# Output projection and SwiGLU FFN in seven quarter products, three blocks of 704 tokens

## The chip, the cores and the metric

The kernel runs on one core of a Trainium2 chip. The time of a run is the device time in microseconds (us) of one execution; the times of the kernel before were 2599.57, 2597.79 and 2597.86 us, median 2597.86. Engines carry the profile's names: PE is the matrix engine (PEld its weight load), DVE the vector engine, ACT the scalar engine, POOL the GpSimd engine, SP the engine whose queue issues the DMAs.

## What is computed

One inference step of a decoder layer: 2048 new positions and 8 x 8 tokens of running sequences, 2112 tokens in all, width 1024. Two mixers fill the 1024 columns of `y` (S5: 512, HGRN2: 512); the change begins behind them:

```
x  = x + concat([y5, yh]) @ w_out                        # 1024 x 1024
h2 = rmsnorm(x, norm_ffn)
x  = x + (silu(h2 @ w_gate) * (h2 @ w_up)) @ w_down      # 1024 x 2816, twice, and 2816 x 1024
y  = rmsnorm(x, norm_final)                              # x * (mean(x*x) + eps) ** -0.5 * g
```

## The kernel before

All activations are feature-major: features on the 128 partitions, tokens along the free axis. Every product of this part is made in three matmuls: an fp32 operand is split in a high part (`hi`, ACT, L226: a copy to fp32r) and the rest (`lo`, L227: POOL or DVE subtracts), and `mm3` (L256 to L263) adds hi x hi, hi x lo and lo x hi in PSUM. Each matmul takes a 128 x 128 weight tile and streams 256, 320 or 512 tokens.

The first part of the program (u projection, S5, HGRN2, GLU) interleaves generators and writes `y_s` in DRAM; the change leaves it alone. The rest goes by the four token blocks of `GROUPS`: 576 tokens (256 and 320), and three of 512. For each block

- `mix(e, b)` loads x and `y_s`, splits y, loads and splits the eight weight units of `w_out` (`load_unit`), and adds eight products to x (L980);
- `norm2` makes the norm: squares (ACT), their sum (DVE), a one-column matmul per 128 tokens (L999) that leaves one number for each token on the partitions, `inv_rms` (L289, L290), which raises these to the power -0.5 on POOL, and `spread` (L297, L301), which multiplies a diagonal with a matrix of ones to bring the result to all partitions; then x * gain * r, and the split of h;
- `ffn` goes over the 22 column units of the FFN in pairs: gate (L1067), silu (L1070), up, the product s (L1081) and its split (L1083, L1084), and `down` of the pair before, added to x (L1055). A weight is loaded and split anew for each block, as units of 128 x 1024, raw tiles from a pool of four buffers (`raw2`);
- `final` makes the last norm and writes yT.

The mix of the next block runs among the last steps of an FFN, and the final norm of a block among the first steps of the next. The POOL power is written so:

```
nc.vector.tensor_scalar(st[:rows, a:b], ss[:rows, a:b], 1.0 / D, EPS, op0=ALU.mult, op1=ALU.add)
nc.gpsimd.tensor_tensor(r[:rows, a:b], st[:rows, a:b], e.mhalf[:rows, 0:b - a], op=ALU.pow)
```

with at most four columns in one instruction. The program is written in program order; the Tile framework's scheduler then fixes one order for each engine, which the chip keeps.

Of the kernel before, what the change touches and what calls it, by code (L numbers as in the profile page):

```python
# [983 lines left out]
def fm_norm(e, x, n, name):
    nc = e.nc
    acc = raw_tile(e, pool=e.nraws, name=f"sq_{name}")[:, :2 * n]
    acc = acc.rearrange("p (k t) -> p k t", t=n)
    for j in range(0, KD, 2):
        if j == 0:
            nc.scalar.activation(acc, x[:, 0:2], AF.Square)  # L990
            continue
        sq = raw_tile(e, pool=e.nraws, name=f"sq_{name}_{j}")[:, :2 * n].rearrange("p (k t) -> p k t", t=n)
        nc.scalar.activation(sq, x[:, j:j + 2], AF.Square)
        nc.vector.tensor_tensor(acc, acc, sq, op=ALU.add)
    tl = tiles_of(0, n)
    ss = e.ps_x.tile([P, 4], F32, tag="x", name=f"ss_{name}")
    for j, (o, w) in enumerate(tl):
        for a in range(2):
            nc.tensor.matmul(ss[:w, j:j + 1], acc[:, a, o:o + w], e.ones[:, 0:1], start=a == 0, stop=a == 1)  # L999
    return ss  # L1000


def norm2(e, b, x1):
    nc = e.nc
    out = []
    for gi, (t0, n) in enumerate(GROUPS[b]):
        x = cols(x1, b, gi)
        r = e.small.tile([P, 4], F32, tag="r", name=f"r_f{t0}")
        inv_rms(e, fm_norm(e, x, n, f"f{t0}"), tiles_of(0, n), r, f"f{t0}")
        pr = spread(e, r, tiles_of(0, n), f"f{t0}")  # L1010
        pcs = pieces_of(n)
        op = []
        for j, (k, nk) in enumerate(pcs):
            raw = raw_tile(e, pool=e.nraws, name=f"h{t0}_{j}")[:, :nk * n].rearrange("p (k t) -> p k t", t=n)
            for i in range(nk):
                nc.vector.scalar_tensor_tensor(raw[:, i], x[:, k + i], e.gain[:, KD + k + i:KD + k + i + 1], pr[:, :n],
                                               op0=ALU.mult, op1=ALU.mult)
            hi, lo = wtile(e, f"h{t0}_{j}", e.ops)
            flat = raw.rearrange("p k t -> p (k t)")
            split(e, flat, hi[:, :nk * n], lo[:, :nk * n], nc.vector if j % 2 else nc.gpsimd)  # L1020
            op.append((hi, lo))
        out.append((t0, n, op_k(op, pcs, n)))
    return out


def final(e, b, x1, parts=None):
# [1 line left out]
    T0 = GROUPS[b][0][0]
    for t0, n in parts or GROUPS[b]:
        x = x1[:, :, t0 - T0:t0 - T0 + n]  # L1030
        r = e.small.tile([P, 4], F32, tag="r", name=f"r_z{t0}")
        inv_rms(e, fm_norm(e, x, n, f"z{t0}"), tiles_of(0, n), r, f"z{t0}")
        pr = spread(e, r, tiles_of(0, n), f"z{t0}")
        for k in range(0, KD, 2):
            raw = raw_tile(e, pool=e.nraws, name=f"z{t0}_{k}")[:, :2 * n].rearrange("p (k t) -> p k t", t=n)
            for i in range(2):
                nc.vector.scalar_tensor_tensor(raw[:, i], x[:, k + i], e.gain[:, 2 * KD + k + i:2 * KD + k + i + 1], pr[:, :n],
                                               op0=ALU.mult, op1=ALU.mult)
            nc.sync.dma_start(fm(e.o["yT"], k, 2, t0, n), raw)
# [284 lines left out]
```

## Time and profile before

| | |
|---|---|
| profiled execution, own time | 2605.76 us |
| its span, first to last instruction | 2604.0 us |
| median of three runs | 2597.86 us |
| granted PE clock, mean | 0.979 of full |
| PE busy | 2493.2 us, 96% of the span |
| POOL busy | 1284.3 us, 49% |
| DVE busy | 950.5 us, 37% |
| ACT busy | 724.2 us, 28% |
| DMA moved | 325.44 MB, mean 125 GB/s |
| chain that ended last | PE 83%, POOL 7%, DVE 3%, DMA 3% |

A busy share is an average over the span. PE's matmuls are pipelined, and the duration of one in the profile is longer than the step from one to the next: the step is read from start times. The chain that ended last follows the work back from the last instruction, at each step to what released it.

### The profile page before, as it was taken

What the parts mean: (1) busy time and instruction counts of PE and PEld (TensorE: products, weight loads), DVE (VectorE), ACT (ScalarE), POOL (GpSimd) and SP (SyncE); (2) the same over time, 40 slices, a digit from 0 to 9 for tenths busy, and PEclk for the clock granted to TensorE, in tenths of its full rate; (3) what the DMA queues carried; (4) which work ended last, traced back from release to release, by engine and by line L of the source; (5) the groups of instructions that cost most, each with busy time, mean ns of one, the idle gap of its engine ahead of it and who ended that gap; (6) DMA issues with size and microseconds to landing.
All of it is one profiled execution on the core that took longest, in us unless ns stands there. A gap on an engine that the chain in (4) does not pass through costs nothing.

```text
span 2604.0 us, 40679 instructions
## 1 busy us (share of the span) xinstructions
PE 2493.2 (96%) x16597; PEld 2141.9 (82%) x16597; DVE 950.5 (37%) x1896; ACT 724.2 (28%) x1161; POOL 1284.3 (49%) x1220
## 2 busy tenths in 40 slices
...
GB/s 266 183 264 199 176 184 167 140 146 124 161 134 169 67 130 114 87 85 89 82 74 101 187 97 98 85 99 92 185 98 112 90 97 97 130 97 97 97 65 33
DMA packets 185966, 325.44 MB, mean 125 GB/s; under 512 B 73642, under 2 KB 109939, under 8 KB 185779
## 3 DMA queue, kind: packets, MB, share of 16 engines
...
q8 instruction: 130, 2.13, 0.3%
q14 instruction: 58, 0.47, 0.1%
...
## 4 chain that ended last, share of the span: by engine, by line
PE 83%; POOL 7%; DVE 3%; DMA 3%; issue 2%; SPq 1%; ACT 1%; POOLq 0%; DVEq 0%; ACTq 0%
PE pu L263 19%; PE pg L263 19%; PE pd L263 19%; PE po L263 7%; PE ps_v L263 3%; PE ps_u L263 2%; PE pz L263 2%; PE ps_f L263 2%; PE ps_g L263 2%; PE ps_q L263 2%; POOL H L802 1%; POOL t L801 1%; POOL t L800 1%; POOL H L803 1%; POOL H L804 1%
## 5 line engine op out<-in xcount | busy, mean ns | idle before, releaser
L1055 DVE TENSOR_TENSOR x<-x,pd 128x512 f32<-128x512 f32 (+1 forms) x448 | 253.1, 585 | 537.4 <-PE pd L263 536.5
L227 POOL TENSOR_TENSOR l_wd<-r_wd,h_wd 128x1024 fp32r<-128x1024 f32 x88 | 215.5, 2448 | 341.9 <-ACT h_wd L226 328.0
L263 PE MATMUL pg<-h_h,h_wg 128*128 128x512 f32 (+2 forms) x880 | 311.7, 354 | 9.3 <-ACT h_wg L226 9.3
L263 PE MATMUL pg<-h_h,l_wg 128*128 128x512 f32 (+2 forms) x880 | 310.9, 354 | 2.2 <-POOL l_wg L227 2.2
L263 PE MATMUL pd<-hl,h_wd 128*128 128x512 f32 (+2 forms) x896 | 312.1, 349 | 0.6 <-POOL hl L1084 0.6
L263 PE MATMUL pd<-hh,l_wd 128*128 128x512 f32 (+2 forms) x896 | 311.7, 349 | 0.0
L263 PE MATMUL pg<-l_h,h_wg 128*128 128x512 f32 (+2 forms) x880 | 310.9, 353 | 0.0
L263 PE MATMUL pu<-h_h,l_wu 128*128 128x512 f32 (+2 forms) x880 | 309.6, 352 | 1.1 <-POOL l_wu L227 1.1
L263 PE MATMUL pu<-h_h,h_wu 128*128 128x512 f32 (+2 forms) x880 | 309.9, 352 | 0.0
L263 PE MATMUL pu<-l_h,h_wu 128*128 128x512 f32 (+2 forms) x880 | 309.8, 352 | 0.0
L227 POOL TENSOR_TENSOR l_wu<-r_wu,h_wu 128x1024 fp32r<-128x1024 f32 x88 | 213.8, 2429 | 182.5 <-ACT h_wu L226 182.5
L263 PE MATMUL pd<-hh,h_wd 128*128 128x512 f32 (+2 forms) x896 | 296.2, 349 | 0.1
L227 POOL TENSOR_TENSOR l_wg<-r_wg,h_wg 128x1024 fp32r<-128x1024 f32 x88 | 213.0, 2420 | 128.1 <-ACT h_wg L226 125.6
L1081 DVE TENSOR_TENSOR s<-s,pu 128x512 f32<-128x512 f32 (+1 forms) x110 | 65.3, 594 | 460.8 <-PE pu L263 457.9
L226 ACT ACTIVATE h_wd<-r_wd 128x1024 fp32r<-128x1024 f32 x88 | 93.5, 1062 | 434.3 <-PE pd L263 290.8
L263 PEld LDWEIGHTS pg<-h_h,h_wg 128*128 128x128 f32 x880 | 167.3, 190 | 29.9 <-ACT h_wg L226 9.5
L263 PEld LDWEIGHTS pd<-hl,h_wd 128*128 128x128 f32 x896 | 169.0, 189 | 21.5 <-POOL hl L1084 0.8
L263 PEld LDWEIGHTS pg<-h_h,l_wg 128*128 128x128 f32 x880 | 167.0, 190 | 23.2 <-POOL l_wg L227 2.6
L263 PEld LDWEIGHTS pd<-hh,h_wd 128*128 128x128 f32 x896 | 168.3, 189 | 21.0 <-ACT hh L1083 0.3
L263 PEld LDWEIGHTS pd<-hh,l_wd 128*128 128x128 f32 x896 | 168.8, 189 | 19.9
L263 PEld LDWEIGHTS pg<-l_h,h_wg 128*128 128x128 f32 x880 | 167.2, 190 | 20.6
L263 PEld LDWEIGHTS pu<-h_h,l_wu 128*128 128x128 f32 x880 | 165.8, 188 | 21.6 <-POOL l_wu L227 1.4
...
## 6 DMA issues: line engine op xcount, KB each, us to landing
r_wg<-in_w_gate_u SPq DMA_DIRECT2D x88, 512.0 KB, 3.3
r_wu<-in_w_up_u SPq DMA_DIRECT2D x88, 512.0 KB, 3.3
r_wd<-in_w_down SPq DMA_DIRECT2D x88, 512.0 KB, 3.2
r_wo<-in_w_out_u SPq DMA_DIRECT2D x32, 512.0 KB, 3.3
xr_u<-in_xr SPq DMA_DIRECT2D x16, 512.0 KB, 5.3
r_xu<-in_xT SPq DMA_DIRECT2D x14, 512.0 KB, 5.4
r_y<-y_s SPq DMA_DIRECT2D x14, 512.0 KB, 5.5
h_v<-wx_s SPq DMA_DIRECT2D x12, 512.0 KB, 4.3
```

The lines of the kernel that those rows point to most:

```text
L226: e.nc.scalar.activation(hi, raw, AF.Copy)
L227: eng.tensor_tensor(lo, raw, hi.bitcast(F32), op=ALU.subtract)
L263: e.nc.tensor.matmul(out, whl[k][a], xhl[k][b], start=start and i == 0, stop=stop and i == len(seq) - 1)
L800: eng.tensor_tensor(t1, prev, ar.to_broadcast(two), op=ALU.mult)
L801: eng.tensor_tensor(t2, prev, ai.to_broadcast(two), op=ALU.mult)
L802: eng.tensor_tensor(dst, dst, t1, op=ALU.add)
L803: eng.tensor_tensor(dst[:, 0], dst[:, 0], t2[:, 1], op=ALU.subtract)
L804: eng.tensor_tensor(dst[:, 1], dst[:, 1], t2[:, 0], op=ALU.add)
L1055: nc.vector.tensor_tensor(x1[:, d, o], x1[:, d, o], ps[:, :n], op=ALU.add)
L1081: nc.vector.tensor_tensor(s[:, :n], s[:, :n], pu[:, :n], op=ALU.mult)
```

## The change

The tokens go in three blocks of FT = 704, each in two halves of FH = 352. `w_out`, `w_gate`, `w_up` and `w_down` are each taken as 2 x 2 quarters: two row tiles of the output (j and j + 4, or two FFN units) by two halves of the contraction, against the two halves of the contraction by the two token halves. Seven products of quarters (the Winograd form of Strassen's scheme) take the place of eight, each with the three matmuls of hi and lo. What this needs:

- `w_prep` loads a raw weight pair into one of two raw tiles (pool `wr`, two buffers), makes four sums on DVE, and splits seven operands of 128 x 512, hi on ACT and lo on POOL, into a ring of `ws` pairs (7, later 10);
- `combine` makes the four sums of the activations on DVE; y, h and s go with their sums to DRAM as seven slots (`ty_s`, `h_s`, `s_s`), and `x_slots` loads and splits them into a ring of X pairs (7, later 8), lo on DVE;
- `seven` runs the products, two matrices in turn, in three PSUM tiles for each matrix (A, Q, B), of which A and B go on summing after a sink has read them; the sinks add to x, or make silu and the product;
- `norm_r` sums the squares with a full 128 x 128 matmul of ones, so that each partition has the sums of all tokens, and raises [128, 704] to the power -0.5 in one POOL instruction. `inv_rms` and `spread` are no longer used here;
- the order of the program: mix of all three blocks with norm2 of the block before in between, then the FFN of the three blocks, with `final` of the block before after 14 of the FFN's steps (two units of gate and up).

The diff, cut:

```diff
+FT = 704
+FH = FT // 2
+CH = [(0, 4), (8, 4), (16, 3)]
...
+def combine(v, t, b11, b12, b21, b22):
+    v.tensor_tensor(t[0], b12, b11, op=ALU.subtract)
+    v.tensor_tensor(t[1], b22, t[0], op=ALU.subtract)
+    v.tensor_tensor(t[2], b22, b12, op=ALU.subtract)
+    v.tensor_tensor(t[3], b21, t[1], op=ALU.subtract)
...
+def x_slots(e, srcs, nk, name):
+    for i, s in enumerate(srcs):
+        raw = e.xraw.tile([P, 4, FH], F32, tag="xr", name=f"xr_{name}_{i}")[:, :nk]
+        nc.sync.dma_start(raw, s)
...
+        nc.scalar.activation(hi, raw, AF.Copy)
+        nc.vector.tensor_tensor(lo, raw, hi.bitcast(F32), op=ALU.subtract)
...
+def w_prep(e, mats, nk):
+        raw = e.wraw.tile([P, 6, 512], F32, tag="wr", name=f"wr_{name}")
+        for fh in range(2):
+            nc.sync.dma_start(raw[:, 2 * fh:2 * fh + 2, :n], srcs[fh].rearrange("p (h f) -> p h f", h=2))
...
+        def sp(src):
+            nc.scalar.activation(hi, src, AF.Copy)
+            nc.gpsimd.tensor_tensor(lo, src, hi.bitcast(F32), op=ALU.subtract)
...
+        v.tensor_tensor(s1, a21, a22, op=ALU.add)
+        v.tensor_tensor(s2, s1, a11, op=ALU.subtract)
...
+        v.tensor_tensor(a12, a12, s2, op=ALU.subtract)
+        v.tensor_tensor(a21, a11, a21, op=ALU.subtract)
...
+def seven(e, mats, X, nk):
+    for i in range(7):
+        for m, (W, sink, name) in enumerate(mats):
+            which = "AQBABAA"[i]
+            first = i < 3
...
+            for k in range(nk):
+                for c, (w, x) in enumerate(((0, 0), (0, 1), (1, 0))):
+                    nc.tensor.matmul(ps, W[i][w][:, ks], X[i][x][:, k], start=first and k == 0 and c == 0,
+                                     stop=i in (1, 4, 6) and k == nk - 1 and c == 2, skip_group_check=True)
+            sink(i, ps)
...
+def up_sink(e, s, name, dst, j):
+        if i == 6:
+            v.tensor_tensor(s[w], s[w], ps, op=ALU.mult)
+            combine(v, T, s["00"], s["01"], s["10"], s["11"])
+            for slot, t in ((0, s["00"]), (1, s["10"]), (2, T[0]), (3, T[1]), (4, s["11"]), (5, T[2]), (6, T[3])):
+                nc.sync.dma_start(dst[:, slot, j], t)
...
+        else:
+            v.tensor_tensor(u[w], u[w], ps, op=ALU.add)
+            v.tensor_tensor(s[w], s[w], u[w], op=ALU.mult)
...
+def norm_r(e, x, name):
...
+        nc.tensor.matmul(ps, e.ones, tot[:, hs], start=True, stop=True)
+        nc.vector.tensor_scalar(r[:, hs], ps, 1.0 / D, EPS, op0=ALU.mult, op1=ALU.add)
+    nc.gpsimd.tensor_tensor(r, r, e.mhalf[:, 0:1].to_broadcast([P, FT]), op=ALU.pow)
...
+        for b in (1, 2):
+            mg = mix(e, b, got[b])
+            run(mg, 7)
+            norm2(e, b - 1, got[b - 1]["x"])
+            run(mg)
+        norm2(e, 2, got[2]["x"])
...
+    for b in range(FB):
+        ff = ffn(e, b, got[b])
+        run(ff, 14)
+        if b:
+            final(e, b - 1, got[b - 1]["x"])
+        run(ff)
+    final(e, FB - 1, got[FB - 1]["x"])
```

In the order of the engines two places matter. The first is POOL's queue at a final norm within an FFN. Before (`l_` and `hl` are the lo parts of weights and of s, `r_z` the power):

```order
L227 TENSOR_TENSOR l_wg_2_17796<-r_wg_2_17793,h_wg_2_17795 128x1024
L1084 TENSOR_TENSOR hl_2_17456<-s_1088_17488,hh_2_17455 128x512
L227 TENSOR_TENSOR l_wd_2_17863<-r_wd_2_17860,h_wd_2_17862 128x1024
L227 TENSOR_TENSOR l_wu_2_17829<-r_wu_2_17826,h_wu_2_17828 128x1024
L1084 TENSOR_TENSOR hl_2_17531<-s_1088_17563,hh_2_17530 128x512
L290 TENSOR_TENSOR r_z_17605<-st_z_17626,mhalf 128x4
L227 TENSOR_TENSOR l_wg_2_17871<-r_wg_2_17868,h_wg_2_17870 128x1024
L227 TENSOR_TENSOR l_wd_2_18002<-r_wd_2_17999,h_wd_2_18001 128x1024
```

and with the change (`wl_g` and `wl_u` are the lo parts of the gate's and the up weight's operands, the second number of a name counts the product from 0 to 6, `wr` is the raw tile):

```order
L1032 TENSOR_TENSOR wl_u_1_2_17082<-wr_u_1_17058,wh_u_1_2_17081 128x512
L1032 TENSOR_TENSOR wl_g_1_3_17086<-wr_g_1_17051,wh_g_1_3_17085 128x512
L1032 TENSOR_TENSOR wl_u_1_3_17092<-wr_u_1_17058,wh_u_1_3_17091 128x512
L1176 TENSOR_TENSOR rr_z_17027<-rr_z_17027,mhalf 128x704
L1032 TENSOR_TENSOR wl_g_1_4_17098<-wr_g_1_17051,wh_g_1_4_17097 128x512
L1032 TENSOR_TENSOR wl_u_1_4_17102<-wr_u_1_17058,wh_u_1_4_17101 128x512
L1032 TENSOR_TENSOR wl_g_1_5_17106<-wr_g_1_17051,wh_g_1_5_17105 128x512
L1032 TENSOR_TENSOR wl_u_1_5_17110<-wr_u_1_17058,wh_u_1_5_17109 128x512
```

The power now has 704 columns in place of 4, and the lo parts of a unit's products 4 to 6 stand behind it. Five of the six powers stand so, among the lo parts of weights (the first within mix of block 1, the second within mix of block 2, the third to fifth within the three FFNs); the sixth is POOL's last instruction.

The second place is DVE's queue behind the first norm2. Before, at a norm2 (`r_h` is x * gain * r, the L1055 rows add `pd` to the x of the block before):

```order
L1081 TENSOR_TENSOR s_1088_19176<-s_1088_19176,pu_1088_19243 128x512
L1016 SCALAR_TENSOR_TENSOR r_h_0_19209<-x_3_18575,gain,rr_f_19204 128x512 x2
L1016 SCALAR_TENSOR_TENSOR r_h_1_19216<-x_3_18575,gain,rr_f_19204 128x512 x2
L227 TENSOR_TENSOR l_h_1_19220<-r_h_1_19216,h_h_1_19219 128x1024
L1016 SCALAR_TENSOR_TENSOR r_h_2_19223<-x_3_18575,gain,rr_f_19204 128x512 x2
L1055 TENSOR_TENSOR x_2_15833<-x_2_15833,pd_1088_0_19312 128x512
```

and with the change (`acc_m` are the tiles of x, `xl_y` the lo part of an X slot, `pA`, `pB` the PSUM tiles of mix of block 1, `ht` the sums of `combine`):

```order
L1009 TENSOR_TENSOR xl_y_0_10870<-xr_y_0_10867,xh_y_0_10869 128x1408
L1091 TENSOR_TENSOR acc_m_10194<-acc_m_10194,pB_o_1_10388 128x352
L1185 SCALAR_TENSOR_TENSOR acc_m_9229<-acc_m_9229,gain,rr_f_10529 128x704
L1185 SCALAR_TENSOR_TENSOR acc_m_9231<-acc_m_9231,gain,rr_f_10529 128x704
L1185 SCALAR_TENSOR_TENSOR acc_m_9233<-acc_m_9233,gain,rr_f_10529 128x704
L1185 SCALAR_TENSOR_TENSOR acc_m_9235<-acc_m_9235,gain,rr_f_10529 128x704
L1185 SCALAR_TENSOR_TENSOR acc_m_9237<-acc_m_9237,gain,rr_f_10529 128x704
L1185 SCALAR_TENSOR_TENSOR acc_m_9239<-acc_m_9239,gain,rr_f_10529 128x704
L1185 SCALAR_TENSOR_TENSOR acc_m_9241<-acc_m_9241,gain,rr_f_10529 128x704
L1185 SCALAR_TENSOR_TENSOR acc_m_9243<-acc_m_9243,gain,rr_f_10529 128x704
L976 TENSOR_TENSOR ht_0_10539<-acc_m_9229 128x352
L978 TENSOR_TENSOR ht_0_10539<-acc_m_9231,acc_m_9229 128x352
```

The eight multiplications that need the power now stand in one run, and the sinks of mix of block 1 from its product 5 on stand behind them.

## Rows read from the trace of the kernel before

**Rows 1.** Busy time by stretch: us; PE, PEld, DVE, ACT, POOL busy (count); clock, DMA share, GB/s
```profile
838.00:2579.00 1741.00, 1714.84 (x9120) 1504.84 (x9120) 465.51 (x739) 471.90 (x584) 878.22 (x434) 0.99 0.30 101
893.00:921.00 28.00, 6.75 (x35) 5.92 (x33) 18.04 (x29) 9.83 (x11) 11.00 (x7) 0.55 0.18 53
921.00:930.00 9.00, 6.77 (x29) 6.37 (x30) 0.61 (x1) 5.66 (x6) 9.00 (x5) 0.51 0.96 350
1420.00:2030.00 610.00, 610.00 (x2726) 506.00 (x2725) 170.84 (x232) 174.03 (x202) 329.25 (x155) 1.00 0.35 117
2579.00:2604.00 25.00, 3.72 (x16) 3.24 (x16) 9.72 (x23) 2.52 (x4) 0.70 (x1) 0.56 0.25 84
```
**Rows 2.** Chain that ended last, in order of time: start us, us, what
```profile
841.17 52.38 PE po L263 x380
...
924.54 8.45 PE pg L263 x44
...
2100.13 5.44 PE pu L263 x24
```
**Rows 3.** Instructions of PE in order of time, GLU: start us, us; 20 steps apart
```profile
709.31 0.32 PE L263 MATMUL pz<-ghi,gwl 128*128 128x352 f32 x1
...
712.53 0.32 PE L263 MATMUL pz<-ghi,gwl 128*128 128x352 f32 x1
```
**Rows 4.** POOL's powers, groups by shape: busy us, mean ns | idle before
```profile
L107 POOL TENSOR_TENSOR dte<-dte,dte 128x16 f32<-128x16 f32 x1 | 2.9, 2911 | 0.4 <-DVE dte L90 0.4
...
L107 POOL TENSOR_TENSOR lbe<-lbe,lbe 128x8 f32<-128x8 f32 x1 | 1.6, 1642 | 1.0 <-DVE lbe L90 1.0
...
L512 POOL TENSOR_TENSOR ss<-rs,mhalf 128x4 f32<-128x4 f32 x16 | 16.6, 1038 | 117.4 <-DVE rs L511 117.3
...
L512 POOL TENSOR_TENSOR ss<-rs,mhalf 64x1 f32<-64x1 f32 x4 | 2.2, 544 | 0.0
```
**Rows 5.** POOL's subtractions and ACT's copies, groups by shape
```profile
L1084 POOL TENSOR_TENSOR hl<-s,hh 128x512 fp32r<-128x512 f32 x66 | 84.9, 1287 | 28.3 <-ACT hh L1083 28.3
...
L1083 ACT ACTIVATE hh<-s 128x512 fp32r<-128x512 f32 x66 | 41.7, 633 | 23.2 <-DVE s L1081 23.2
...
L931 ACT ACTIVATE ghi<-gg 128x1408 fp32r<-128x1408 f32 x6 | 8.3, 1382 | 18.6 <-DMA gg<-g_s 18.6
```
**Rows 6.** DVE, groups by shape
```profile
L994 DVE TENSOR_TENSOR r_sq_z<-r_sq_z,r_sq_z 128x512 f32<-128x512 f32 x9 | 6.2, 689 | 5.8 <-ACT r_sq_z L993 5.8
...
L227 DVE TENSOR_TENSOR l_xu<-r_xu,h_xu 128x1024 fp32r<-128x1024 f32 x7 | 8.5, 1219 | 0.1
...
L1016 DVE SCALAR_TENSOR_TENSOR r_h<-x,gain,rr_f 128x512 f32<-128x512 f32 x24 | 16.5, 744 | 7.1 <-PE rr_f L301 7.1
```
**Rows 7.** POOL and DVE in order of time about 900 and 918 us: start us, us
```profile
899.91 2.35 POOL L227 TENSOR_TENSOR l_h<-r_h,h_h 128x1024 fp32r<-128x1024 f32 x1 [4.60 <-ACT h_h L226]
...
918.84 3.34 POOL L227 TENSOR_TENSOR l_y<-r_y,h_y 128x1024 fp32r<-128x1024 f32 x1
...
900.23 2.71 DVE L994 TENSOR_TENSOR r_sq_f<-r_sq_f,r_sq_f 128x640 f32<-128x640 f32 x1
...
904.00 1.74 DVE L994 TENSOR_TENSOR r_sq_f<-r_sq_f,r_sq_f 128x640 f32<-128x640 f32 x2
...
918.12 1.83 DVE L227 TENSOR_TENSOR l_y<-r_y,h_y 128x1024 fp32r<-128x1024 f32 x1 [0.64 <-ACT h_y L226]
```
**Rows 8.** POOL's power and a DVE instruction beside it: start us, us
```profile
48.43 2.90 POOL L107 TENSOR_TENSOR mge<-mge,mge 128x16 f32<-128x16 f32 x1 [6.77 <-DVE scs L122]
...
50.39 0.17 DVE L98 TENSOR_TENSOR mge<-mge,mge 128x16 f32<-128x16 f32 x1
```
**Rows 9.** DMA issues: count, KB each, median us from issue to landing
```profile
r_wg<-in_w_gate_u SPq DMA_DIRECT2D x88, 512.0 KB, 3.3
...
r_y<-y_s SPq DMA_DIRECT2D x14, 512.0 KB, 5.5
...
x<-in_xT SPq DMA_DIRECT2D x3, 2048.0 KB, 9.0
```

More of the change, by code (lines that the diff above doesn't have):

```diff
@@ L984, in fm_norm @@
[L984 to L1000, printed above, removed]
@@ L1003, in norm2, with __init__, set, pick @@
-def norm2(e, b, x1):
+FT = 704
+FH = FT // 2
+FB = TOK // FT
+CH = [(0, 4), (8, 4), (16, 3)]
+class Rot:
+    def __init__(self, *pools):
+        self.set(*pools)
+    def set(self, *pools):
+        self.order = [p for p, n in pools for _ in range(n)]
+        self.i = 0
+    def pick(self):
+        self.i += 1
+        return self.order[(self.i - 1) % len(self.order)]
+    def tile(self, *a, **k):
+        return self.pick().tile(*a, **k)
+def combine(v, t, b11, b12, b21, b22):
[3 more added lines that the diff above has]
+    v.tensor_tensor(t[3], b21, t[1], op=ALU.subtract)
@@ L1004, in norm2, with y_slots @@
+def y_slots(e, b):
+    t0 = b * FT
+    t = e.ty_s[b]
+    return [fm(e.y_s, 0, 4, t0, FH), fm(e.y_s, 4, 4, t0, FH), t[:, 0], t[:, 1], fm(e.y_s, 4, 4, t0 + FH, FH), t[:, 2], t[:, 3]]
+def x_slots(e, srcs, nk, name):
     nc = e.nc
     out = []
[L1006 to L1022, printed above, removed]
@@ L1027, in final @@
     nc = e.nc
[L1028 to L1039, printed above, removed]
@@ new lines, in pool_tag, with acc_sink, sink, gate_sink @@
+def pool_tag(e, pool):
+    p = pool.order[pool.i % len(pool.order)]
+    return e.tags[p]
+def acc_sink(e, x0, x1):
+    q = [x0[:, :FH], x0[:, :FH], x1[:, FH:], x0[:, FH:], x0[:, FH:], x1[:, FH:], x1[:, :FH]]
+    def sink(i, ps):
+        e.nc.vector.tensor_tensor(q[i], q[i], ps, op=ALU.add)
+    return sink
+def gate_sink(e, s, name):
+    nc = e.nc
+    which = ["00", "00", "11", "01", "01", "11", "10"]
+    def sink(i, ps):
+        w = which[i]
+        if w not in s:
+            s[w] = e.hp.tile([P, FH], F32, tag="s", name=f"s{w}_{name}")
+            nc.scalar.activation(s[w], ps, AF.Silu if i == 6 else AF.Copy)
+        else:
+            nc.vector.tensor_tensor(s[w], s[w], ps, op=ALU.add)
+            nc.scalar.activation(s[w], s[w], AF.Silu)
+    return sink
@@ new lines, in acc_tiles, with mix @@
+def acc_tiles(e, b, src, name):
+    x = {}
+    for j in range(4):
+        for d in (j, j + 4):
+            x[d] = e.acc.tile([P, FT], F32, tag="acc", name=f"acc{d}_{name}")
+            e.nc.sync.dma_start(x[d], src[d * P:(d + 1) * P, b * FT:(b + 1) * FT])
+    return x
+def mix(e, b, got):
+    x = acc_tiles(e, b, e.i["xT"], f"m{b}")
+    got["x"] = x
+    X = x_slots(e, y_slots(e, b), 4, f"y{b}")
+    for g in range(2):
+        js = (2 * g, 2 * g + 1)
+        W = w_prep(e, [([e.i["w_out_u"][d] for d in (j, j + 4)], f"wo{j}_{b}") for j in js], 4)
+        mats = [(w, acc_sink(e, x[j], x[j + 4]), f"o{j}_{b}") for w, j in zip(W, js)]
+        for _ in seven(e, mats, X, 4):
+            yield
+    for d in range(KD):
+        e.nc.sync.dma_start(e.x1_s[d * P:(d + 1) * P, b * FT:(b + 1) * FT], x[d])
```

299 lines of the change are left out of this document (159 added, 140 removed).

## The prediction

> **What bounds the kernel now.** I read the page first (PE 96% of the span and 83% of the chain that ended last), then the busy time by stretch. From 838 us on the output projection and the FFN run to 2579 us [rows 1]. Within it, 1420 to 2030 us has PE busy for 610.0 of 610.0 us: PE is never waiting there, while POOL is busy for 329 us and DVE for 171. The stretch holds one hole, 893 to 921 us, the first norm (PE 6.75 of 28 us), and 25 us stand behind the last product: the last norm and its stores. So PE sets the time, the other engines are cover, and this change takes work from PE and gives it to the cover.
>
> What a matmul costs is its step, not its duration. 24 matmuls of 512 tokens take 5.44 us [rows 2], 0.2267 us each; 380 of 256 and 320 tokens take 52.38 us, 0.1378 each; 20 steps of 352 tokens, the shape that the change uses, take 712.53 - 709.31 = 3.22 us [rows 3], 0.161 each.
>
> **What the change removes.** Before, a token group needs 8 x 8 x 3 + 3 x 22 x 8 x 3 = 1776 matmuls; three groups of 512 and two of 256 and 320 (the few of the last `down` that are cut in two counted whole) make 5328 x 0.2267 + 3552 x 0.1378 = 1697 us. After, seven products x nk x 3 for each pair: 84 matmuls at nk = 4. Six pairs of mix, 33 of gate and up at two matrices each, 12 of down, and six of down at nk = 3 (126 matmuls) make 51 x 168 + 6 x 126 = 9324, times 0.161 = 1501 us. That is **196 us less on PE**. The stretch of 1741 us [rows 1] held 1697 us of these, so 44 us of holes go too; what comes in their place is counted below. The 838 us ahead stay: mix of block 0 is now behind the mixers, as it was: it begins at 841 us [rows 2].
>
> **The power.** This term decides. `norm_r` raises 704 columns on POOL where `inv_rms` raised at most four. The groups by shape give 544 ns for 1 column, 1038 for 4, 1642 for 8 and 2911 for 16 [rows 4]: (2911 - 1642) / 8 = 159 ns, (1642 - 1038) / 4 = 151 ns, (2911 - 544) / 15 = 158 ns for each further column, with no sign of bending. The trace shows no wide power. Its bounds: from below the price of a POOL subtraction of the same width, 1287 ns for 512 [rows 5], so 1.8 us; from above the straight line, 0.386 + 704 x 0.158 = **111 us**. I take the line, since four widths lie on it and the lower end is another operation.
>
> Six such powers run. Five stand in POOL's queue ahead of lo parts without which no product can start (the first excerpt of the order). PE can go on only with what is already split: the ring holds ten operands, so at most ten products x 12 x 0.161 = 19 us, at least nothing. I take 8 us, since below POOL has no lead. On DVE the eight multiplications wait for the power too, and sinks and raw sums stand behind them (the second excerpt). What each norm adds on POOL's and DVE's common path: seven sums of 704 at 689 x 704 / 512 = 0.95 us, 6.6 us, and eight multiplications at 744 x 704 / 512 = 1.02 us, 8.2 us [rows 6]; norm2 has 16 sums of 352 more, 0.47 us each, 7.6 us. So a norm2 costs 111 + 22 - 8 = 125 us, a `final` 111 + 14 - 8 = 117: 3 x 125 + 2 x 117 = **609 us**; with full cover and half of DVE's work hidden 507, with none 649. The sixth power stands in the tail: sums 6, matmul and scale 2, power 111, multiplications 8, store 5, together 132 us in place of 25, **107 more**. Each halt also lets the clock fall: over 893 to 930 us the granted clock is 0.55 and 0.51 [rows 1], about the 1.2 GHz level, and the first 44 matmuls behind it take 8.45 us against 44 x 0.1378 = 6.1 [rows 2]; five times 2.4 is **12 us**.
>
> **The common port of POOL and DVE.** A DVE sum of two SBUF tiles and a POOL subtraction do not run at once. A sum of 640 columns takes 1.74 / 2 = 0.87 us alone, and 2.71 when a subtraction had begun 0.32 us before it: the rest of that subtraction, 2.35 - 0.32, and its own 0.87 make 2.9. It goes the other way as well: `l_y` took 3.34 us on POOL behind a DVE subtraction, against 2.35 [rows 7]. Now add up one unit of gate and up, which PE does in 168 x 0.161 = 27.0 us. POOL: 14 subtractions x 1.287 = 18.0 us [rows 5]. DVE, two-SBUF instructions alone: eight sums of 512 x 0.689 [rows 6] and seven of 352 x 0.47, 8.8 us. Together 26.8: no room. And POOL pauses once a unit, since `wr` has two buffers: a raw tile is free only after its seventh subtraction, then 1 MB has to land (3.3 us for 512 KB, 9.0 for 2048 KB [rows 9], so 5.2 by the line between), and ACT must copy (0.63, [rows 5]): 4.6 us after the 1.29 us that the other matrix covers. So a unit takes between 27.0 us (the pause filled with DVE's part, PE the bound) and 31.5. I take 30.6, as most of DVE's 8.8 us hangs on the raw tile or on PE and can't fill the pause: 3.6 x 33 = 119 us. `down` at nk = 4 has 18.0 + 5.5 and half of seven X slots, 3.5 x 1219 x 1408 / 1024 = 5.9: 29.4 to 34 us, I take 32.6, 5.6 x 12 = 67; at nk = 3, three quarters of that and 4 of pause, 22 to 26 against 20.3, I take 25.6, 5.3 x 6 = 32; mix and the X slots of h, 37. Sum **255 us**, with both ends 0 and 375.
>
> The Trainium skill (SBUF — State Buffer, Who interferes with whom) states this exclusion as a lock that is held for the whole instruction: a DVE instruction with two SBUF inputs against a GpSimd instruction that reads SBUF. On the subtractions the trace agrees, 2.71 us against 0.87.
>
> **The start of mix.** Before the first product of block 0, X slots come through one raw buffer: load 5.5 us for 512 KB, so 6.3 for 720 KB [rows 9], copy 1.38 [rows 5], subtraction 1.68: 9.3 us a slot, 65 for seven, where PE needs 27: **38 us** (15 to 60). The same feed of block 1, with 32 sums of `combine_y`, lies beside the first power and costs nothing while that lasts 111 us; without it some 40 us would show. ACT has room: 14 copies x 0.63 and ten shorter ones in 27 us a unit. SP's queue holds the stores of each norm's results, with raw loads behind them; it stands still under a power, at no further cost, since no raw tile gets free while POOL is at it.
>
> **Sum**, against the profiled execution's own time: 2605.8 - 196 - 44 + 609 + 107 + 12 + 255 + 38 = 3386.8. That execution is 7.9 us above the median of the runs shown, so **3380 us**, 30% slower.
>
> By the Trainium skill (TensorE: Matmul & The Clock Gate, Wait — 56ns, not 53.3ns?) a warm matmul starts every N / 2.4 GHz + 2.5 ns, 149 ns for 352 columns; the sum would be lower by 9324 x 12 ns = 112 us, 3268 us. The row of this very shape shows 161, so I stay with it.
>
> **Rivals.**
> *PE stays the bound.* The same powers, but POOL and DVE interleave so well that nothing but the powers holds PE, and ten products are split when each begins: 2605.8 - 196 - 44 + 507 + 107 + 12 + 38 - 7.9 = 3022 us. For it: POOL's 18.0 us a unit alone fit in 27.0. Against it: the 26.8 us of both.
> *The power stops DVE.* If it held the port as a subtraction does, DVE's two-SBUF work would not pass beside it: the sums of `combine_y` (16 us) and seven X slots (12) move behind the first power, and some 5.5 us behind each of four others, 50 us: 3430. Against it: under a power of 16 columns from 48.43 to 51.33 us, a DVE instruction of two SBUF tiles at 50.39 takes 0.17 us [rows 8]. By the same section of the Trainium skill (SBUF — State Buffer, Who interferes with whom) this would follow for any GpSimd instruction that reads SBUF; on this row the trace does not agree.
> *The wide power is cheap, and PE the bound* (the other side). If POOL's power over 704 columns ran near its lower bound, no halt would be left and the tail would be 23 us: 2605.8 - 196 - 44 + 38 + 25 - 2 - 7.9 = 2419 us (25: DVE's part of five norms, 5 us each left uncovered), 7% faster. It turns at (2598 - 2419) / 6 = 30 us a power, 42 ns a column, against 158 measured at narrow widths. With the port's 255 us as well it would be 2674, slower in spite of it.
>
> **How the numbers follow.** Forecast 0.62, PE the bound 0.18, the power stops DVE 0.08, cheap power and PE the bound 0.05, cheap power with the port 0.03, dearer than all of these (both upper ends) 0.04. The forecast's own range runs from 3200 (a third of the port's term) to 3500 (its upper end 375). The range reaches down to the first rival: 3000 to 3500; outside lie the cheap powers, the dearest case and the edges. A difference of 0.2% (5 us) is about what a measurement of this kernel tells from none: faster 0.05, same 0.01, slower 0.94.
>
> **What would show it.** Right: six POOL rows of L1176 near 111 us each; PE idle for 90 us or more beside five of them, released by an L1032 subtraction, with POOL at 100% there; a tail of some 130 us; L1076 steps of 0.161 us; POOL and DVE sums that take up to 2 us where they meet, and PE short of busy within FFN units away from the powers, waiting for L1032. Wrong: L1176 rows of a few us (then the third rival), or PE full between the powers (then the first). The whole prediction falls if a wide power costs less per column than a narrow one.

## The result, and the profile after

The changed kernel takes 3360.65 us, median of four runs (3355.69 to 3370.24), against 2598.72 for the kernel before: ratio 1.2933, 95% interval 1.2901 to 1.2966, 29% slower. The forecast was 3380 in a range of 3000 to 3500. The profiled execution took 3370.24 us with a span of 3368.5.

The page of the changed kernel first: busy time, the slices of PE, POOL and the clock, and the chain that ended last.

```profile
PE 2398.2 (71%) x16813; PEld 2210.8 (66%) x16813; DVE 2269.8 (67%) x2692; ACT 996.7 (30%) x1848; POOL 2300.7 (68%) x1587
...
PE   7989999997713705029999985298998816898840
...
POOL 4176585511587698866667778976767797666778
PEclk9999999998856857559999998599999957999975
...
PE 30%; DVE 21%; POOL 19%; DMA 12%; issue 10%; POOLq 3%; ACT 2%; SPq 1%; DVEq 0%; ACTq 0%
...
L1176 POOL TENSOR_TENSOR rr_z<-rr_z,mhalf 128x704 f32<-128x704 f32 x3 | 338.0, 112665 | 18.5 <-DVE rr_z L1175 18.5
L1176 POOL TENSOR_TENSOR rr_f<-rr_f,mhalf 128x704 f32<-128x704 f32 x3 | 337.9, 112625 | 10.9 <-DVE rr_f L1175 10.9
```

PE fell from 96% of the span to 71%, and from 83% of the chain to 30%. The six powers take 112.6 us each; the straight line through widths 1 to 16 [rows 4] had given 111.

Busy time by stretch (us; PE, PEld, DVE, ACT, POOL busy with counts; clock, DMA share, GB/s): the first and the third power, a stretch of FFN units without one, the fourth power, and the tail.

```profile
950.00:1063.00 113.00, 0.00 (x0) 0.00 (x0) 87.93 (x17) 0.00 (x0) 112.38 (x1) 0.50 0.18 59
1362.00:1475.00 113.00, 0.00 (x0) 0.00 (x0) 83.81 (x3) 0.00 (x0) 113.00 (x2) 0.52 0.00 0
1550.00:1825.00 275.00, 254.48 (x1525) 251.60 (x1525) 197.73 (x203) 118.01 (x221) 187.78 (x126) 0.97 0.36 128
2058.00:2171.00 113.00, 20.41 (x112) 19.83 (x110) 85.09 (x8) 6.53 (x14) 113.00 (x3) 0.59 0.02 9
3238.40:3368.50 130.10, 2.40 (x4) 0.80 (x4) 11.08 (x14) 1.36 (x2) 112.47 (x1) 0.52 0.06 22
```

Where PE was full from 1420 to 2030 us [rows 1], it now has 0 to 20 us of work under a power, and away from the powers 254 of 275 us. DVE shows 84 to 88 us of work under the first, the third and the fourth power, and most of that is no work. DVE and POOL in order of time under the first power:

```profile
952.53 80.26 DVE L976 TENSOR_TENSOR ct<-cy 128x352 f32<-128x352 f32 x1 [1.99 <-DMA cy<-y_s]
1032.82 0.52 DVE L977 TENSOR_TENSOR ct<-cy,ct 128x352 f32<-128x352 f32 x1
```
```profile
950.62 112.48 POOL L1176 TENSOR_TENSOR rr_f<-rr_f,mhalf 128x704 f32<-128x704 f32 x1 [7.25 <-DVE rr_f L1175]
```

A DVE sum of two SBUF tiles, 0.52 us long elsewhere, stands still from 952.53 to 1032.79 us, 82.2 us after the power began, and then DVE runs freely for the last 30 us of the same power. The other four powers within the mix and the FFN show the same: the sum that DVE has begun is released 82.3 to 82.8 us after the power began. Beside the sixth, in the tail, DVE has no such sum in its queue.

Now one stop within the units. DVE, then POOL, then PE about 1590 to 1602 us:

```profile
1590.85 0.96 DVE L1037 TENSOR_TENSOR wr_u<-wr_u 128x512 f32<-128x512 f32 x1 [2.65 <-DMA wr_u<-in_w_up_u]
1591.85 1.67 DVE L1038 TENSOR_TENSOR wr_u<-wr_u 128x512 f32<-128x512 f32 x1
1593.44 1.78 DVE L1045 TENSOR_TENSOR wr_u<-wr_u 128x512 f32<-128x512 f32 x1
1595.14 1.77 DVE L1044 TENSOR_TENSOR wr_g<-wr_g 128x512 f32<-128x512 f32 x1
1596.84 0.51 DVE L1105 TENSOR_TENSOR s<-s,pB_g 128x352 f32<-128x352 f32 x1
...
1600.91 0.51 DVE L1105 TENSOR_TENSOR s<-s,pA_g 128x352 f32<-128x352 f32 x1
```
```profile
1591.22 1.75 POOL L1032 TENSOR_TENSOR wl_g<-wr_g,wh_g 128x512 fp32r<-128x512 f32 x1
1592.93 1.74 POOL L1032 TENSOR_TENSOR wl_u<-wr_u,wh_u 128x512 fp32r<-128x512 f32 x1
1594.63 1.73 POOL L1032 TENSOR_TENSOR wl_g<-wr_g,wh_g 128x512 fp32r<-128x512 f32 x1
```
```profile
1601.47 0.43 PE L1076 MATMUL pA_g<-xh_h,wh_g 128*128 128x352 f32 x1 [1.85 <-DVE s L1105]
```

POOL's subtractions (1.29 alone [rows 5]) and DVE's sums (0.69 alone) take turns at 1.7 us each. The sink of `pA_g`, which reads PSUM and is not slowed itself (0.51), stands behind them in DVE's queue, and PE, which goes on adding to the same PSUM tile, waits 1.85 us for it. Such sinks are what PE waits for in the units; all its waits from 1524 to 1825 us (total, times, longest):

```profile
PE pA_g L1076 <- DVE s L1105: 21.4, 10, 3.7
PE pA_u L1076 <- DVE u L1128: 1.3, 1, 1.3
```

In what follows a *unit* is the 168 matmuls of one pair of gate and up, measured from its first start to the next unit's; away from the powers its mean is 31.26 us over 30 units, 32.2 for `down` at nk = 4 and 22.3 at nk = 3, where PE alone would need 26.7 and 20.0.

### The profile page after: what moved, and what is told of

It is laid out like the page before. It is cut to its first block, busy times and chain, and to the rows that moved or that the text cites. A ratio compares the mean times of both kernels' runs of the same rounds, so it can differ in the third digit from the quotient of the medians.

```text
span 3368.5 us, 44865 instructions
## 1 busy us (share of the span) xinstructions
PE 2398.2 (71%) x16813; PEld 2210.8 (66%) x16813; DVE 2269.8 (67%) x2692; ACT 996.7 (30%) x1848; POOL 2300.7 (68%) x1587
## 4 chain that ended last, share of the span: by engine, by line
PE 30%; DVE 21%; POOL 19%; DMA 12%; issue 10%; POOLq 3%; ACT 2%; SPq 1%; DVEq 0%; ACTq 0%
POOL rr_f L1176 7%; PE pA_u L1076 4%; POOLq L1448 3%; POOL rr_z L1176 3%; PE pA_g L1076 3%; DMA wr_u<-in_w_up_u 3%; PE pA_d L1076 3%; DVE ct L976 2%; DMA wr_wd<-in_w_down_u 2%; POOL wl_wd L1032 2%; PE ps_v L263 2%; PE ps_u L263 2%; DVE s L1129 2%; PE ps_f L263 1%; PE pQ_g L1076 1%
## 5 line engine op out<-in xcount | busy, mean ns | idle before, releaser
L1032 POOL TENSOR_TENSOR wl_u<-wr_u,wh_u 128x512 fp32r<-128x512 f32 x231 | 354.9, 1541 | 198.5 <-ACT wh_u L1031 154.6
L1032 POOL TENSOR_TENSOR wl_wd<-wr_wd,wh_wd 128x512 fp32r<-128x512 f32 (+1 forms) x252 | 382.7, 1545 | 151.9 <-ACT wh_wd L1031 137.8
L1032 POOL TENSOR_TENSOR wl_g<-wr_g,wh_g 128x512 fp32r<-128x512 f32 x231 | 353.0, 1531 | 140.4 <-ACT wh_g L1031 136.2
L1176 POOL TENSOR_TENSOR rr_z<-rr_z,mhalf 128x704 f32<-128x704 f32 x3 | 338.0, 112665 | 18.5 <-DVE rr_z L1175 18.5
L1176 POOL TENSOR_TENSOR rr_f<-rr_f,mhalf 128x704 f32<-128x704 f32 x3 | 337.9, 112625 | 10.9 <-DVE rr_f L1175 10.9
L1076 PE MATMUL pA_g<-xh_h,wh_g 128*128 128x352 f32 x528 | 186.1, 352 | 220.5 <-ACT s L1103 137.2
L1076 PE MATMUL pA_g<-xh_h,wl_g 128*128 128x352 f32 x528 | 182.1, 345 | 98.8 <-POOL wl_g L1032 98.8
L1032 POOL TENSOR_TENSOR wl_wo<-wr_wo,wh_wo 128x512 fp32r<-128x512 f32 x84 | 143.1, 1731 | 109.2 <-ACT wh_wo L1031 100.2
L1076 PE MATMUL pA_d<-xh_s,wh_wd 128*128 128x352 f32 x528 | 179.7, 340 | 44.3 <-DVE acc_d L1091 44.1
L1129 DVE TENSOR_TENSOR s<-s,u 128x352 f32<-128x352 f32 x99 | 183.0, 1849 | 11.9 <-ACT s L1106 6.1
L1076 PE MATMUL pA_g<-xl_h,wh_g 128*128 128x352 f32 x528 | 180.5, 342 | 0.0
```

The lines of the kernel that those rows point to most:

```text
L1032: nc.gpsimd.tensor_tensor(lo, src, hi.bitcast(F32), op=ALU.subtract)
L1076: nc.tensor.matmul(ps, W[i][w][:, ks], X[i][x][:, k], start=first and k == 0 and c == 0, stop=i in (1, 4, 6) and k == nk - 1 and c == 2, s ...
L1129: v.tensor_tensor(s[w], s[w], u[w], op=ALU.mult)
L1176: nc.gpsimd.tensor_tensor(r, r, e.mhalf[:, 0:1].to_broadcast([P, FT]), op=ALU.pow)
```

## The experiments

My theory: the power halts PE by POOL's own time, and the common port of POOL and DVE (the prediction's name for their taking turns) makes the units longer. Rivals: DVE's stop under the power; the pause for the raw tile; POOL's own time in the units.

**narrow.** In `norm_r`, with `tot` the sums over the eight tiles:

```diff
-        nc.tensor.matmul(ps, e.ones, tot[:, hs], start=True, stop=True)
...
-    nc.gpsimd.tensor_tensor(r, r, e.mhalf[:, 0:1].to_broadcast([P, FT]), op=ALU.pow)
+    for c in range(8):
+        nc.tensor.matmul(ps[:R, c:c + 1], tot[:, c * R:c * R + R], e.ones[:, 0:1], start=True, stop=True)
...
+    nc.gpsimd.tensor_tensor(rn[:R], st[:R], e.mhalf[:R, 0:8], op=ALU.pow)
...
+        nc.tensor.matmul(ps, e.ones[:R], dg[:R, hs], start=True, stop=True)
+        nc.scalar.activation(r[:, hs], ps, AF.Copy)
```

> The six powers over 704 columns become powers of 88 x 8: one-column matmuls leave the token sums on 88 partitions, POOL raises eight columns, and a diagonal with a matrix of ones spreads the result again. All else stays. Theory 'the power is the halt': a power of 8 columns takes 1.6 us, the five halts (some 584 us above the mean unit) shrink to under 15 us each and the tail from 119 to about 30 us: 2700 to 2760 us. Rival 'the halts hide work that POOL and DVE owe anyway' (weights and sums that would have to be caught up): only part comes back, 2850 to 3000 us. Rival 'without the power PE is full' (the units are slow because of the powers): 2420 to 2500 us, faster than the kernel before.

Measured: 2752.83 us, ratio to before 1.0578 (1.0546 to 1.061), in the theory's range. 608 us came back. A power takes 1.63 to 2.02 us; the tail is 23.5 us (it was 130 by the row above; the 119 of the expectation was a miscount). The two `final` within the FFN cost 1 to 2 us each over a mean unit. The three norm2 do not fall under 15 us: 65 us remain behind the first mix, 36 in the third mix, 34 in the first FFN unit. Of the 65, 59 lie at one place, from the start of a product to the start of the next (1.9 us where nothing stops PE; stops below are counted in the same way), and they end with ACT's copy of the next block's X, which is loaded through the buffers that the sums of its y hold until then. The units stay at 31.0, `down` at 32.3, so the powers were not what made these slow, and the rival "without the power PE is full" is out.

**before_wide.** The wide power alone, in the kernel before: the same ones-product and one power per group of 256, 320 or 512 tokens, in place of `inv_rms` and `spread`, in `norm2` and `final`.

```diff
-        inv_rms(e, fm_norm(e, x, n, f"f{t0}"), tiles_of(0, n), r, f"f{t0}")
-        pr = spread(e, r, tiles_of(0, n), f"f{t0}")
+        pr = wide_r(e, x, n, f"f{t0}")
```

> One part of the change alone: the kernel before, all products as they were, but the norms of the output projection's stretch and the last norms summed by a full ones-product and raised to the power in one POOL instruction of 256, 320 or 512 columns. By 0.27 us + 0.1595 us a column the eleven powers take 678 us of POOL. Theory 'the power is the halt, with or without the seven products': PE goes on only as long as split weights last, 5 to 20 us of cover each: 3050 to 3230 us, so that most of the change's loss appears without any seven-product. Rival 'PE's stock and POOL's idle half cover it' (POOL is busy for 49% before): 2650 to 2800 us.

Measured: 3151.78 us, 1.2116 (1.2089 to 1.2142): 552 us more than before, with no seven-product in it. POOL's powers, groups by line, and PE's longest wait:

```profile
L1019 POOL TENSOR_TENSOR rw_z<-rw_z,mhalf 128x256 f32<-128x256 f32 (+2 forms) x6 | 338.5, 56420 | 24.0 <-DVE rw_z L1018 24.0
L1019 POOL TENSOR_TENSOR rw_f<-rw_f,mhalf 128x512 f32<-128x512 f32 (+2 forms) x5 | 338.2, 67639 | 19.6 <-DVE rw_f L1018 19.6
```
```profile
PE pg L263 <- POOL l_wg L227: 218.5, 5, 54.9
```

That lies in the theory's range, 3050 to 3230. 677 us of power cost 552: by the difference, some 11 us of each of the eleven were covered on average.

**chunk88.** Each power in eight pieces:

```diff
-    nc.gpsimd.tensor_tensor(r, r, e.mhalf[:, 0:1].to_broadcast([P, FT]), op=ALU.pow)
+    for w in [88] * 8:
+        nc.gpsimd.tensor_tensor(r[:, a:a + w], r[:, a:a + w], e.mhalf[:, 0:1].to_broadcast([P, w]), op=ALU.pow)
+        a += w
```

> Each power over 704 columns is issued as eight powers of 88 columns. The sum by the line is 8 x (0.386 + 88 x 0.158) = 114 us a norm, so POOL is held as long. Theory 'the halt is POOL's own time': 3340 to 3380 us, no change. Rival 'DVE's stop of 82 us under each power is what costs': a DVE sum waits at most about 14 us, the sums of the second block's y and of the weights pass beside the power, and 40 to 60 us come back: 3300 to 3320 us.

Measured: 3341.33 us, 1.2837 (1.2811 to 1.2864), some 20 us less than with whole powers. A piece takes 14.36 us, eight of them 114.9. The six pairs of mix took 455 us in place of 484, most of it in the second and third (181 in place of 205), and began 9 us later; the three FFN units with a power took 448 in both. So both theories hold a part: DVE's stop costs, but only about the first mix, where the sums of y stand behind it, and some 20 us in all where the rival had 40 to 60. Elsewhere POOL holds PE anyway.

**widths.** The powers in pieces of different width (640 + 64, 512 + 192, 448 + 256; 352 + 352, 256 + 256 + 192; 704).

> The powers are issued in pieces: 640 + 64, 512 + 192, 448 + 256 in the three norm2, 352 + 352 and 256 + 256 + 192 in two of the final norms, 704 in the last; with 704, a DVE sum of two SBUF tiles stood still until 82 of 112.5 us. Theory a, the last 192 columns leave DVE free: a piece of 640 holds it for 448 columns (71 us), 512 for 320 (51), 448 for 256 (41), 352 for 160 (26), 256 for 64 (10), 192 and 64 not at all. Theory b, a piece of the first 512 columns holds it: 640 for 512 columns (81 us), 512 and all below for their whole time. Theory c, a fixed share of 0.73: 640 for 74 us, 512 for 59, 352 for 41, 192 for 22. Time as with the powers whole, 3340 to 3400 us.

A single run, 3373.01 us. POOL's and DVE's instructions in order of time, at a piece of 640 columns and at one of 512:

```profile
957.03 102.34 POOL L1178 TENSOR_TENSOR rr_f<-rr_f,mhalf 128x640 f32<-128x640 f32 x1 [7.25 <-DVE rr_f L1175]
...
1181.07 81.91 POOL L1178 TENSOR_TENSOR rr_f<-rr_f,mhalf 128x512 f32<-128x512 f32 x1 [3.48 <-DVE rr_f L1175]
```
```profile
958.69 80.41 DVE L976 TENSOR_TENSOR ct<-cy 128x352 f32<-128x352 f32 x1 [1.74 <-DMA cy<-y_s]
...
1186.66 0.68 DVE L1037 TENSOR_TENSOR wr_wo<-wr_wo 128x512 f32<-128x512 f32 x1
1187.38 0.69 DVE L1038 TENSOR_TENSOR wr_wo<-wr_wo 128x512 f32<-128x512 f32 x1
```

None of the three theories is right as it stood. The piece of 640 holds DVE until 1039.10 us, 82.1 us after its start, as the 704 did: the time of 512 columns (81.9). The piece of 512 doesn't hold it: sums of two SBUF tiles run 5.6 us after its start in their usual 0.69 us. At the same place of the program, 5.55 us into the whole power of 704 columns, the same sum was held:

```profile
1181.25 76.78 DVE L1037 TENSOR_TENSOR wr_wo<-wr_wo 128x512 f32<-128x512 f32 x1
```

Beside the pieces of 352 and 256, and the 88 of chunk88, such sums run at their usual pace from 2 us after the start on. So the powers of 640 and 704 columns hold DVE's two-tile sums while their first 512 are worked, and those of 512 and fewer don't, apart from the first 2 us where a row shows these. For 512 this rests on one power of one execution, beside the pieces of 448 and 192 no such sum began, and no width between 512 and 640 was run. The rows don't show why.

**narrow_raw3.** On the narrow powers: `wr` with a third buffer, the ring of operands cut from ten to eight to make room.

> The narrow powers, and a third raw weight tile; the ring of operands goes from ten to eight to make room. Theory 'the units are slow because POOL pauses for its raw tile' (10 us of idle POOL time a unit, ended by the copy behind a load): units of gate and up fall from 31 to 27 or 28 us and those of down from 32 to 28, some 130 us less than with the narrow powers alone. Rival 'the common port': POOL's 18 us and DVE's 8.8 fill the 27, units stay at 30 to 31 and the time within 30 us of the narrow powers.

Measured: 2732.51 us, 1.0507 (1.0489 to 1.0526). Units fell from 31.0 to 29.7, just under the rival's 30 to 31, `down` rose from 32.3 to 33.7, 20 us in all: the pause is a small part, and the rival stands. The shorter ring, cut in the same run, may cost something in the units too, but little: plain2 below, with the lo parts shared, also has a ring of eight, and its units stay within 0.1 us of plain1's.

**lo3.** On the narrow powers, three of each matrix's seven lo parts go to DVE:

```diff
-            nc.gpsimd.tensor_tensor(lo, src, hi.bitcast(F32), op=ALU.subtract)
+            (nc.vector if len(ops) in (0, 1, 6) else nc.gpsimd).tensor_tensor(lo, src, hi.bitcast(F32), op=ALU.subtract)
```

> The narrow powers, and the lo parts of three of a matrix's seven operands (the first two and the last) are subtracted on DVE, 6 of 14 a unit; POOL keeps 8. Theory 'the common port' (POOL's subtractions stretch DVE's sums from 0.69 to 1.7 us, the sinks stand behind them and PE waits for a sink): a lo part takes about 0.65 us on DVE against 1.29 on POOL, the port's load of a unit falls from 26.8 to 10.3 + 12.7 = 23 us, units of gate and up from 31.0 to 27.5 to 28.5, down from 32.3 to 29, mix a little: 2590 to 2650 us against 2753 with the narrow powers alone. Rival 'the raw tile's pause' (a unit waits for its load, whoever subtracts): units stay at 30 to 31, and the longer queue of DVE makes them worse if anything: 2740 to 2790 us.

Measured: 2639.06 us, 1.0161 (1.0134 to 1.0188), 114 us less, in the theory's range. A lo part takes 0.69 us on DVE (median). Units fell to 28.8, a little less far than the theory's 28.5, `down` to 29.9. DVE got more work and still delivers its sinks earlier; PE's waits over the whole run with the narrow powers, and with lo3:

```profile
PE pA_g L1076 <- DVE s L1105: 74.9, 31, 4.8
...
PE pA_d L1076 <- DVE acc_d L1091: 46.0, 24, 4.3
```
```profile
PE pA_g L1076 <- DVE s L1105: 30.5, 19, 4.8
...
PE pA_d L1076 <- DVE acc_d L1091: 23.5, 16, 3.7
```

The eight weight sums of a unit, 5.5 us by their duration alone, took 9.7 us of DVE with the narrow powers and 7.1 here.

**nosum.** On the narrow powers, the weights' sums left out (the edit is the four lines of `w_prep` that add and subtract, and the operands taken from the raw quarters).

> The narrow powers, and DVE's four sums of each weight matrix left out (eight a unit): the operands are split from the raw quarters, so the products are not the reference's; POOL still makes all 14 lo parts of a unit, ACT all copies, PE all products, and a raw tile is held as before. Theory 'the common port' (POOL's 18 us and DVE's two-SBUF work share it; DVE's sinks come late behind the stretched sums): with DVE's 5.5 us of sums gone the port's load is 21 us, POOL's subtractions fall from 1.53 us towards 1.3, PE's waits for a sink go from 121 us in all to under 60, units of gate and up from 31 to 28 or 29: 2640 to 2680 us. Rival 'POOL's own time' (14 subtractions and the pause for the raw tile): the units stay within 0.7 us, 2730 to 2770 us.

Measured: 2569.23 us, 0.9883 (0.9845 to 0.992), 184 us less, and more than either theory had. Most units take 27.0 to 27.1 us, PE's own time at 0.161 a matmul, and PE's wait for `s` is gone, while POOL changed little, 1.56 to 1.44 us a subtraction; its subtractions with the narrow powers, and without the sums:

```profile
L1032 POOL TENSOR_TENSOR wl_g<-wr_g,wh_g 128x512 fp32r<-128x512 f32 x231 | 360.7, 1564 | 145.9 <-ACT wh_g L1031 140.5 <-PE pA_u L1076 4.7 <-DMA acc_d<-x_s 0.6
```
```profile
L1032 POOL TENSOR_TENSOR wl_g<-wr_g,wh_g 128x512 fp32r<-128x512 f32 x231 | 331.9, 1438 | 140.9 <-ACT wh_g L1031 140.2 <-PE pA_o L1072 0.4
```

POOL, with its pause of some 4 us a matrix (140 us over 33 units), had room all along. What is short is DVE's queue: the sums themselves, their stretching by the port and their wait for a load, all ahead of sinks. This run takes the three away together, and how the 184 us divide among them isn't shown.

**lo3_raw3**, both edits, and **lo3_raw3_order**, which also moves the third block's y sums behind the second mix's first pair and loads the first FFN's X slots ahead of the last norm2.

> Both: six of the 14 lo parts on DVE, and three raw weight tiles with a ring of eight operands. Theory 'the port first, then the raw tile': with the port relieved the third raw tile takes the last waits, units near 27 us, 2560 to 2610 us. Theory 'port alone': the same as with the six lo parts on DVE within 15 us. Rival 'the smaller ring': eight operands in place of ten cost more than the raw tile brings, 10 to 30 us slower than without it.

> As the one before, and two pieces moved in program order: the sums of the third block's y come after the second mix has begun and not ahead of it, and the first FFN's X slots are loaded ahead of the last norm2. The halt behind the first mix, 59 us with the narrow powers, is 8 rounds of about 8 us through two buffers; with four rounds gone it should be near 27, and the halt of 29 us in the first FFN unit should go to 5 to 15: some 45 us less than without the moves, 2500 to 2560 us, faster than the kernel before by 2 to 4%. Rival 'the loads of the next mix only wait elsewhere': the four rounds turn up ahead of the third mix, and under 15 us come back.

Measured: 2648.93 us, 1.0187 (1.0165 to 1.0208): with the port relieved the shorter ring costs as much as the raw tile brings or more, 10 us in all against lo3 (units 28.4 against 28.8, `down` 31.2 against 29.9). And 2632.37 us, 1.0124 (1.0107 to 1.014): the halt behind the first mix fell from 58 to 19 us, and 26 us turned up ahead of the third, as the rival said; 17 us came back.

**best1.** Lo parts as in lo3, y sums in place over five buffers, three buffers for norm2's sums.

> Narrow powers, six of 14 lo parts on DVE, two raw tiles, a ring of eight; the sums of y are made in place and rotate over five buffers in place of two, the third block's after the second mix has begun; the first FFN's X slots ahead of the last norm2, whose sums have three buffers in place of one (PE waited 23 us in the first FFN unit for a sink tile in memory that these held). Theory 'what is left of the halts are waits for these buffers': the 19 and 26 us about the second mix fall under 10 each, the one in the first FFN unit from 40 to 15 to 25, some 40 us less than 2632: 2580 to 2610 us, level with the kernel before or up to 1% faster. Rival 'the loads and their landing, not the buffers': 2620 to 2650 us, still slower than before.

Measured: 2628.16 us, 1.0111 (1.0092 to 1.013). The halt behind the first mix went, but 28 us came in the second and 27 in the first FFN unit: the time lies in the rival's range, so more buffers alone don't take these stops away.

**plain1** and **plain2.** On lo3 and the X slots' move: the projection back to eight quarter products.

```diff
-    X = x_slots(e, y_slots(e, b), 4, f"y{b}")
+    X = x_slots(e, [fm(e.y_s, 4 * kh, 4, t0 + th * FH, FH) for th in range(2) for kh in range(2)], 4, f"y{b}")
...
-        for _ in seven(e, mats, X, 4):
+        for _ in eight(e, W, x, js, X, b):
...
-            combine_y(e, 0, cp)
```

> Narrow powers, six of 14 lo parts of the FFN on DVE, the first FFN's X slots ahead of the last norm2, and the output projection put back to eight quarter products in blocks of 704: four X slots straight from y, four operands a matrix without sums, no sums of y through DRAM. PE's part of the projection goes from 6 x 26.7 to 6 x 30.6 us, 23 us more. Theory 'in the projection the seven products do not pay, since the sums of y and seven slots a block stand ahead of PE': its six pairs, 287 us with the narrow powers and six lo parts on DVE, fall to 200 to 220, the halts of 59 and 20 us go, and the time to 2530 to 2580 us, faster than the kernel before by 1 to 3%. Rival 'the halts belong to the norms': they stay, and the time is 2630 to 2660 us.

> As the one before, with a ring of eight weight operands in place of ten and three buffers in place of one for the sums of norm2. Theory 'the sums' buffer': the wait in the first FFN unit falls by 10 to 15 us and outweighs the shorter ring, 10 us faster than with one buffer. Theory 'the ring': down's units get 1 us longer each, 5 to 15 us slower.

Measured: plain1 2530.01 us, 0.9737 (0.9721 to 0.9752); plain2 2540.14, 0.978 (0.9759 to 0.9802), so the ring counts for more than the buffers. The mixes and the FFN of plain1 by stretch (columns as above):

```profile
818.00:1023.00 205.00, 198.34 (x1235) 195.42 (x1236) 120.50 (x146) 76.57 (x110) 86.80 (x56) 0.98 0.66 232
1023.00:2503.00 1480.00, 1374.48 (x8364) 1353.68 (x8363) 1200.79 (x1577) 650.71 (x1143) 614.39 (x406) 0.97 0.43 149
```

The projection begins at 818.6 us in place of 853.4 (lo3), with no sums of y through DRAM ahead of it and four X slots in place of seven, and its six pairs take 204 us in place of 287, with PE busy for 198 of 205. So in the projection seven products cost more than they save. For the FFN, eight products in blocks of 704 were not run; by the step of 0.161 us they would need 192 x 0.161 = 30.9 us of PE alone for a unit (an estimate), and plain1's units behind the first have a mean of 28.9, so there seven pay, with the narrow power and the lo parts shared. The whole is 2.6% faster than the kernel before. Not all of that is the FFN's: of the 76 us between the two profiled executions 23 lie ahead of the projection, which began at 841.17 us in the kernel before.

## Why the prediction was right, and where it was off

| term of the sum | forecast, us | measured, us |
|---|---|---|
| up to the first product, and the first pair's feed | 838 + 38 | 848 + 26 |
| 9324 matmuls | 1501 | 1483 (0.159 each) |
| five halts, with the clock behind them | 609 + 12 | 626 |
| units, gate and up / `down` nk 4 / nk 3 / mix | 119 / 67 / 32 / 37 | 150 / 66 / 14 / 26 |
| tail | 132 | 130 |

The measured column adds up to 3369, the span. A halt is the length of the pair or unit in which the power falls, less that of a pair at PE's pace (mix) or of a mean unit (FFN). The terms agree better than their parts: of the five halts and of the units some came out over and some under the forecast, so that their sums hit within 5 us and 1 us is luck.

- *The power* was right: 112.6 us against 111, six rows, and it decides: narrow gives 608 of the 762 us back, and the wide power alone costs the old kernel 552. The line through narrow widths held out to 704.
- *The halts* were right in sum and off in their parts. The three norm2 cost 137, 135 and 150 us where I had 125, the two `final` 102 and 103 where I had 117. In the former, more stood behind: the y sums after the first, and after the third the sink tiles of the FFN (136 us of PE's wait ended with ACT's L1103), as narrow leaves 65 and 34 us there without a wide power. That L1103 was itself released by DVE's sums of h (`ht`) at 1496 us, 21 us after the power ended: two rounds of these waited 4.6 and 4.4 us for the store of an earlier one, where my sum had 7.6 us for all of them and no wait. "Released by an L1032 subtraction" failed for four of the five: the last to end were copies of X (114.5 us), DVE's sinks (77.3), ACT's sinks (136.0 and 70.2), and once L1032 (97.0).
- *"The power stops DVE"*, put at 0.08 on the row of 16 columns [rows 8], was half the case: a narrow power doesn't stop DVE and a wide one does, for 82 of 112.5 us. Its price was 50; chunk88 gives some 20. The Trainium skill (SBUF — State Buffer, Who interferes with whom) has a GpSimd instruction that reads SBUF contend with any DVE instruction of two SBUF inputs; the traces agree for the subtractions (0.69 us becomes up to 1.78) and for the first 512 columns of a wider power (82.1 us), not for powers of 512 columns and fewer (0.68 to 0.69 us beside the 512).
- *The port* came out at 256 us against 255, and that is luck: its mechanism was wrong in part, and the 256 hold slow-clock steps that the term had left out. The prediction added POOL and DVE up to 26.8 of 27.0 us and had PE wait for L1032. That the two slow each other was right, but PE waits for DVE's sinks instead; POOL has room (nosum). The pause of the raw tile, which made 3.6 us a unit in my sum, is worth about 1.3 (narrow_raw3).
- *The clock* was mis-sized where it isn't a halt. From the starts of all 9324 matmuls, steps between 0.2 and 0.36 us cost 91 us more than 0.159 would: some 20 in the five pairs and units in which a power begins (the forecast had 12), 30 in the 30 units away from the powers, the rest in mix and `down`, where the forecast had nothing. Rows of PE behind the third halt and 3 us later:

```profile
1499.54 0.50 PE L1076 MATMUL pA_g<-xh_h,wh_g 128*128 128x352 f32 x1
1499.83 0.50 PE L1076 MATMUL pA_g<-xl_h,wh_g 128*128 128x352 f32 x1
...
1502.58 0.32 PE L1076 MATMUL pA_u<-xh_h,wl_u 128*128 128x352 f32 x1
1502.73 0.32 PE L1076 MATMUL pA_u<-xh_h,wh_u 128*128 128x352 f32 x1
```

  The step is 0.29 us at first and 0.16 then, the two levels of 1.2 and 2.4 GHz. Short stops do it too, but not each time: behind the third halt, of 37 steps of 1.6 to 3.2 us 12 are followed by six or more slow ones. A product at the slow step takes 3.5 us in place of 1.9.
- *The matmul's step* of 161 ns was right against the 149, an estimate by the formula of the Trainium skill (TensorE: Matmul & The Clock Gate, Wait — 56ns, not 53.3ns?): 9324 matmuls at full clock go at 159 to 161 ns.
